# A Hyena and SwiGLU encoder layer: reordering the joint between the output projection and the first SwiGLU pair

## The chip, the core and the metric

The kernel runs on one core of one Trainium2 chip. The metric is the device time of one execution in microseconds; a kernel's time is the median of several runs. TensorE does matmuls and transposes, VectorE elementwise work on two operands, ScalarE activations and copies, GpSimd (POOL in the profile) elementwise work on SBUF and the issue of software DMAs, SyncE (SP) the issue of the other DMAs.

## The reference, cut to what matters

One layer (DEPTH is 1) over 1024 tokens of width 1024, in float32:

```
h = rmsnorm(x, norm_mix)
z = short_conv(h @ w_in + b_in, conv_w, conv_b);  x0, x1, v = split(z, 3)
s = v * x1
y = fft_convolution(s, implicit_filter) + s * skip
x = x + (y * x0) @ w_out + b_out
x = x + (silu(n @ w_gate) * (n @ w_up)) @ w_down      # n = rmsnorm(x, norm_ffn)
out = rmsnorm(x, norm_final)
```

The hidden width of the SwiGLU part is 2816.

## The kernel before, in words

**Numbers.** Every large matmul is done in three products of rounded parts. An operand is split into a high part (a cast to fp32r) and a low part (the value less the high part), and the terms (high, high), (high, low), (low, high) are summed in PSUM (`TERMS`). A low part is made in one of three ways: a subtraction on VectorE; a subtraction on GpSimd; or `low_dma` (L148 to L150): ScalarE writes minus the high part to the low tile, then POOL's queue issues a DMA that adds the source onto it. `split_dma` (L152) is the cast and then `low_dma`; `early_op` (L1302) calls it for a weight.

**Output projection.** `wos[h][k // 2]` are the split weights of column half h, `u2[part][th]` the split input, one K tile k of 128 rows each. `out_part(m, ks, terms)` (L925) adds the K tiles ks to the first column half of row tiles m and m + 4. K tiles 0 to 5 are done in an earlier stretch; K tile 6 (the seventh) is done at L1008 to L1012 with `inverse_mm` of the last Hyena block between its pieces; tile 7 closes. Within the seventh K tile each row tile's three terms follow one another, and the second term reads the low part of weights `wos[0][3]`, a `low_dma`.

**The loop of the joint (L1310).** It goes over the second column half in the order of rows `seq = (0, 4, 1, 5, 2, 3, 6, 7)`. Step n: TensorE computes the half for row tile j = seq[n] (24 matmuls), then transposes row tile seq[n-1] (`turn`, L1292; the result, `tp`, lies in one of two PSUM tiles). VectorE and ScalarE do, in this order: `x1_half(j)` (L1035: add to x1, square with sum on ScalarE, store to `xd` on SP's queue); `post_late()`, what the step before left over; `normed(j)` (L1078: `norm_begin` L1063 and `norm_end` L1068, which scales both halves of x1 in place; the second half must wait until the store of L1045 has read it); `post(seq[n-1])`, the split of the transposed tile.

**The split of a transposed tile.** Rows 0 to 3 are left tiles (`top_left`, L1091): ScalarE casts the high part from PSUM to u2, copies the tile to x1, and for tiles 0 to 2 `low_dma` makes the low part; for tile 3 VectorE subtracts it, in `post_late`. Rows 4 to 7 are right tiles (class `Right`, L1103): besides their own parts T4 and B22 they give the sums T1, T2, T3 of a Strassen scheme, each split (`high`, `low`). For rows 4 and 5 `top_sums` (L1166) does all of it in the loop; for rows 6 and 7 (`r6`, `r7`) the steps are written out after the loop.

**The SwiGLU units.** A `Unit` (L1197) is one block of 256 columns of the gate (`ug`) or up weights (`uu_`): four raw quarters a11, a12, a21, a22, loaded on SP into slots that x1 tiles 0, 1, 4 and 5 held, sums s0 to s3 of them, and seven products of 12 matmuls: a (p1) and b (p2) into pa, f into pb, g into pc, e into pd, then d on top of pc and c on top of pd. pc and pd are the halves of one PSUM tile, `dc`. `p1_out` (L1249) copies pa to SBUF on ScalarE before p2 adds to it. `w_op` (L1191) splits a weight operand with ScalarE and VectorE. `end_products` (L1274) first adds pd to a running sum (L1275) and then calls for d and c; `end_sums` reads all of dc.

**The joint after the loop (L1347 to L1408)** is a hand-written order of r6, r7, both first units and `normed(7)`. The early weight parts are `pre` (a11 of both units) and `pq` (a12 of both).

**What sets the order.** In the joint the order of TensorE, VectorE and ScalarE is the program's own (`manual_schedule`, L1306). SP and POOL are ordered there by the framework's planner; up to L1051 they are by hand too. Every queue works in order.

Of the kernel before, what the change touches and what calls it, by code (L numbers as in the profile page):

```python
# [13 lines left out]
ALU = mybir.AluOpType  # L14
# [88 lines left out]
def hyena_ffn_kernel(ctx: ExitStack, tc: tile.TileContext, a: dict, out: bass.AP):  # L103
# [15 lines left out]
    def slot(tag, name, shape=(1024,), dt=F32):  # L119
        return sb.tile([P, *shape], dt, tag=tag, name=name)  # L120
# [27 lines left out]
    def low_dma(hi, lo, src):  # L148
        S.activation(lo, hi.bitcast(F32), AF.Copy, scale=-1.0)  # L149
        G.dma_start(lo.bitcast(F32), src, accum_op=ALU.add)  # L150
# [774 lines left out]
    def out_part(m, ks, terms=range(len(TERMS))):  # L925
        for k in ks:
            for q, j in enumerate(PAIRS[m]):
                out_mm(po[m][:, q * 512 : (q + 1) * 512], 0, j, k, terms)
# [76 lines left out]
    wo_load(1, 3, "hs")  # L1005
    wo_split(1, 1)
    x1_load(5)
    out_part(0, (6,))  # L1008
    out_part(1, (6,), (0, 1))
    inverse_mm(b)  # L1010
    out_part(1, (6,), (2,))
    out_part(2, (6,))  # L1012
    finish(b)
    gate(b)
# [63 lines left out]
    def normed(j):  # L1078
        norm_begin(j)
        norm_end(j)  # L1080
# [10 lines left out]
    def top_left(m, pt):  # L1091
        ms = cols_of(m)
        S.copy(u2[0][0][:, :, ms], pt)
        xt = x1[m].rearrange("p (k m) -> p k m", k=NB)
        S.copy(xt, pt)
        if m < 3:
            low_dma(u2[0][0][:, :, ms], u2[1][0][:, :, ms], xt)
            return lambda: None
        return lambda: V.tensor_tensor(
            u2[1][0][:, :, ms], pt, u2[0][0][:, :, ms].bitcast(F32), ALU.subtract  # L1100
        )
# [95 lines left out]
    class Unit:  # L1197
# [54 lines left out]
        def p2(u, t=None, ks=range(4)):  # L1252
            u.product(u.pa, "b", u.a12, "B21", False, t, ks)

        def sums(u, eng):
            eng.tensor_tensor(u.s[0], u.a21, u.a22, ALU.add)
            eng.tensor_tensor(u.s[1], u.s[0], u.a11, ALU.subtract)

        def sum3(u):
            V.tensor_tensor(u.s[2], u.a11, u.a21, ALU.subtract)  # L1260
# [31 lines left out]
    def turn(j):  # L1292
        turns[j] = turned(j)
# [4 lines left out]
    def post_late():  # L1298
        while late:
            late.pop(0)()  # L1300

    def early_op(t, src):  # L1302
        split_dma(t[:, 0], t[:, 1], src)
        return t

    with tc.manual_schedule(  # L1306
        engines={mybir.EngineType.PE, mybir.EngineType.DVE, mybir.EngineType.Activation}
    ):
        pts = {}
        for n, j in enumerate(seq):  # L1310
            if n % 4 < 2:
                pts[n % 2] = mm_psum(f"po1{n}")
            hf = n // 2 % 2
            o = pts[n % 2][:, hf * 512 : (hf + 1) * 512]
            for k in range(NB):
                out_mm(o, 1, j, k)
            if n == 1:
                t_op("T1", "ab_g", ("gg0",))
                t_op("T2", "cr", ("fwd01",))
                t_op("T3", "whl1", ("hs", "wt"))  # L1320
            if 1 <= n <= 6:
                turn(seq[n - 1])
            if n == 7:
                turn(6)
                pq = slot("ss", "pq", (2, 2, 4, P), F32R)
                early_op(pq[:, 0], ug.a12)
            x1_half(j, 1, o)
            if n == 6:
                early_op(pre[:, 1], uu_.a11)
            if n < 7:  # L1330
                post_late()
                normed(j)
            if 1 <= n <= 6:
                post(seq[n - 1])
            if n == 3:
                ug = Unit(0, wg, "wg")
            if n == 4:
                uu_ = Unit(0, wu, "wu")
                pre = slot("whl0", "pre", (2, 2, 4, P), F32R)
            if n == 5:  # L1340
                early_op(pre[:, 0], ug.a11)
            if n == 6:
                post_late()
                ug.s_tag = "ab_d"
                ug.split_sum_tiles()
                ug.sums(V)
        ug.begin(True)  # L1347
        uu_.begin(True)
        r6 = Right(2, turns[6])
        r6.sums12()  # L1350
        norm_begin(7)
        r6.sum3()
        r6.high("T2")
        r6.b22_high()
        norm_end(7)
        ug.p1(pre[:, 0])
        r6.high("T3")
        r6.low("T3", None)
        early_op(pq[:, 1], uu_.a12)
        r6.low("T2", V)  # L1360
        r6.b22_low()
        ug.p1_out()
        ug.early = {"f": w_op("wg0f", ug.s[1])}
        uu_.p1(pre[:, 1])
        turn(7)
        r6.sum4()
        r6.high("T1")
        r6.low("T1", None)
        uu_.p1_out()
        r7 = Right(3, turns[7])  # L1370
        r7.sums12()
        r7.sum3()
        ug.p2(pq[:, 0])
        uu_.p2(pq[:, 1], (0, 1))
        r6.t4_high()
        r6.t4_low(None)
        r7.part("T2", V)
        r7.part("T3", V)
        ug.sum3()
        ug.early["g"] = w_op("wg0g", ug.s[2])  # L1380
        r7.part("T1", V)
        r7.sum4()
        ug.early["e"] = w_op("wg0e", ug.s[0])
        ug.product(ug.pb, "f", None, "T2", True, ug.early["f"])
        V.tensor_tensor(ug.uu[:, 1], ug.uu[:, 0], ug.pb, ALU.add)
        r7.t4_high()
        r7.t4_low(None)
        r7.b22_high()
        r7.b22_low()
        ug.product(ug.pc, "g", None, "T3", True, ug.early["g"])  # L1390
        uu_.p2(pq[:, 1], (2, 3))
        V.tensor_tensor(ug.uu[:, 2], ug.uu[:, 1], ug.pc, ALU.add)
        ug.product(ug.pd, "e", None, "T1", True, ug.early["e"])
        ug.sum4()
        g0 = slot("inv", "g0", (4, 512))
        ug.early["d"] = w_op("wg0d", ug.a22)
        uu_.sum_tiles()
        uu_.sums(V)
        uu_.early["f"] = w_op("wu0f", uu_.s[1])
        ug.end_products(g0[:, 1:4])  # L1400
        uu_.sum3()
        uu_.early["g"] = w_op("wu0g", uu_.s[2])
        S.activation(g0[:, 0], ug.pa, AF.Silu)
        ug.end_sums(g0[:, 1:4])
        uu_.sum4()
        uu_.product(uu_.pb, "f", None, "T2", True, uu_.early["f"])
        V.tensor_tensor(uu_.uu[:, 1], uu_.uu[:, 0], uu_.pb, ALU.add)
        uu_.product(uu_.pc, "g", None, "T3", True, uu_.early["g"])  # L1408

    held = []  # L1410
# [1 line left out]
    def pair(i, ug=None, uu_=None):  # L1412
        early = ug is not None
        g = g0 if early else slot("inv", f"g{i}", (4, 512))
        if not early:
            ug = Unit(i, wg, "wg")
            ug.begin()
            ug.p1()
            ug.p1_out()
            ug.sums(V)  # L1420
            ug.middle()
            ug.p2()
            S.activation(g[:, 0], ug.pa, AF.Silu)
            ug.end(g[:, 1:4])
        S.activation(g[:, 1:4], g[:, 1:4], AF.Silu)
        if not early:
            uu_ = Unit(i, wu, "wu")
            uu_.begin()
            uu_.p1()
            uu_.p1_out()  # L1430
            uu_.sums(V)
            uu_.middle()
            uu_.p2()
        else:
            uu_.middle(True)
        uc = slot("whl0", f"uc{i}", (3, 512))
        V.tensor_tensor(g[:, 0], g[:, 0], uu_.pa, ALU.mult)  # L1437
        uu_.end(uc, early)
        V.tensor_tensor(g[:, 1:4], g[:, 1:4], uc, ALU.mult)
        inner(i, g, store)  # L1440
# [16 lines left out]
    def last_pair(i):  # L1457
        g = slot("inv", f"g{i}", (4, 512))
        ug, uu = Unit(i, wg, "wg"), Unit(i, wu, "wu")
        ug.begin()  # L1460
        uu.begin()
        ug.p1()
        ug.p1_out()
        ug.sums(V)
        uu.p1()
        uu.p1_out()
        ug.product(ug.pb, "f", ug.s[1], "T2", True)
        V.tensor_tensor(ug.uu[:, 1], ug.uu[:, 0], ug.pb, ALU.add)
        ug.sum3()
        ug.product(ug.pc, "g", ug.s[2], "T3", True)  # L1470
        V.tensor_tensor(ug.uu[:, 2], ug.uu[:, 1], ug.pc, ALU.add)
        ug.p2()
        S.activation(g[:, 0], ug.pa, AF.Silu)
        ug.product(ug.pd, "e", ug.s[0], "T1", True)
        uu.sums(V)
        uu.product(uu.pb, "f", uu.s[1], "T2", True)
        V.tensor_tensor(uu.uu[:, 1], uu.uu[:, 0], uu.pb, ALU.add)
        ug.end(g[:, 1:4])
        S.activation(g[:, 1:4], g[:, 1:4], AF.Silu)
        uu.sum3()  # L1480
        uu.product(uu.pc, "g", uu.s[2], "T3", True)
        V.tensor_tensor(uu.uu[:, 2], uu.uu[:, 1], uu.pc, ALU.add)
        uu.p2()
        V.tensor_tensor(g[:, 0], g[:, 0], uu.pa, ALU.mult)
        uu.product(uu.pd, "e", uu.s[0], "T1", True)
        uc = slot("whl0", f"uc{i}", (3, 512))
        uu.end(uc)
        V.tensor_tensor(g[:, 1:4], g[:, 1:4], uc, ALU.mult)
        inner(i, g, lambda *x: held.append(x))
# [211 lines left out]
```

## Time and profile before

| what | value |
|---|---|
| median of 3 runs (lowest to highest) | 1176.32 us (1175.88 to 1178.87) |
| time of the profiled execution | 1177.2 us |
| its span, first to last instruction | 1175.4 us |
| mean granted TensorE clock | 0.996 |
| ScalarE busy, share of the span | 44% |
| DMA moved | 172.95 MB, mean 147 GB/s |

The profile is one execution. A row of the timeline gives start, duration, engine, line, operation, output and inputs, shape and count; in brackets stands how long the engine had been idle before it and what released it. A row of the waits gives an engine and its instruction, what it waited for, the total, how often, and the longest. The row of a window gives, after its ends and its length, for each engine the busy time and the number of instructions, then the granted clock, the share of the DMA engines and GB/s. A row of DMA issues gives the queue, the count, the size and the median time to landing. "PEld" is TensorE's weight load, "SPq" and "POOLq" the issuing queues.

### The profile page before, as it was taken

Reading aid. Unit: us, or ns where it says so; the run is one execution under the profiler, and the core shown is the slowest. Engines: PE = TensorE matmul, PEld = TensorE weight load, DVE = VectorE, ACT = ScalarE, POOL = GpSimd, SP = SyncE. Lnnn points to the kernel's source line nnn. Section 1 sums busy time; section 2 is a strip of 40 time slices with the busy share of each in tenths; the row PEclk is TensorE's granted clock in tenths of the full one; section 3 lists DMA queues with packets and bytes.
Section 4 is the critical chain, followed back from the end, with each engine's and each line's share of the span. In section 5 each row is a group of like instructions: output and inputs, shape, how many; then the busy total and the mean of one; then the engine's idle time right before and its main releaser. Section 6 shows DMA issues by size and latency. Waiting matters only on the chain.

```text
span 1175.4 us, 15154 instructions
## 1 busy us (share of the span) xinstructions
PE 1151.6 (98%) x5714; PEld 970.0 (83%) x5714; DVE 870.8 (74%) x1389; ACT 522.3 (44%) x829; POOL 155.1 (13%) x218
## 2 busy tenths in 40 slices
PE   8999999999999999988999999999999999999997
PEld 6889898898988888876888888888888788788886
DVE  7688989889898895477756676666566567955675
ACT  8563553545446474365333233323333243334445
POOL 0010211112011141052001110111011110110100
PEclk9999999999999999999999999999999999999999
DMA  7456778776674799576223332324133269833323
GB/s 240 145 120 144 141 163 170 159 166 155 129 161 100 195 245 298 148 138 105 96 101 120 105 115 69 130 90 135 56 124 108 75 231 374 297 117 96 99 81 144
DMA packets 105818, 172.95 MB, mean 147 GB/s; under 512 B 7181, under 2 KB 65933, under 8 KB 105616
## 3 DMA queue, kind: packets, MB, share of 16 engines
q0 software_dynamic: 30080, 81.02, 30.5%
q1 hardware_dynamic: 75517, 90.70, 23.3%
q8 instruction: 45, 0.74, 0.2%
q10 hardware_dynamic: 146, 0.27, 0.1%
q14 instruction: 30, 0.24, 0.1%
HBM read 101.96 MB, written 40.11 MB: 121 GB/s over the span
## 4 chain that ended last, share of the span: by engine, by line
PE 85%; DVE 7%; DMA 6%; ACT 1%; issue 1%; POOL 0%; DVEq 0%; POOLq 0%; ACTq 0%; SPq 0%
PE z L140 20%; PE bx L1560 8%; PE po L914 3%; PE bz L1560 3%; PE by L1560 3%; PE pg L541 2%; PE pp L614 2%; PE pg L540 2%; DMA wd<-in_ffn_w_down_dram 2%; DMA xd<-x 1%; DMA wohl<-wo 1%; PE py L653 1%; PE py L654 1%; PE z L366 1%; PE z L693 1%; PE wu9dc L1237 1%
## 5 line engine op out<-in xcount | busy, mean ns | idle before, releaser
L140 PE MATMUL z<-uh,whl 128*128 128x512 f32 x704 | 195.4, 392 | 0.0
L140 PEld LDWEIGHTS z<-uh,whl 128*128 128x128 f32 x704 | 130.1, 188 | 25.6
L1560 PE MATMUL bx<-wop,hop 128*128 128x512 f32 x480 | 110.1, 389 | 0.8 <-DVE hop L130 0.8
L140 PE MATMUL z<-ul,whl 128*128 128x512 f32 x352 | 108.8, 390 | 0.0
L1560 PEld LDWEIGHTS bx<-wop,hop 128*128 128x128 f32 x480 | 90.0, 188 | 19.9 <-DVE hop L130 1.2
L130 DVE TENSOR_TENSOR hop<-hrp,hop 128x1024 fp32r<-128x1024 f32 (+1 forms) x40 | 45.0, 1130 | 52.3 <-ACT hop L129 52.3
L129 ACT CAST hop<-hrp 128x1024 fp32r<-128x1024 f32 (+1 forms) x40 | 38.9, 977 | 96.9 <-PE bx L1560 32.5
L140 PEld LDWEIGHTS z<-ul,whl 128*128 128x128 f32 x352 | 66.1, 188 | 14.1
L914 PE MATMUL po<-wohl,uh 128*128 128x512 f32 x256 | 75.1, 397 | 0.8 <-DMA wohl<-wo 0.7
L1030 POOL DMA_DIRECT2D hd<-g x40 | 21.6, 543 | 320.2 <-DVE g L1437 188.3
L1560 PE MATMUL by<-wop,hop 128*128 128x512 f32 x264 | 60.2, 389 | 0.0
L1560 PEld LDWEIGHTS by<-wop,hop 128*128 128x128 f32 x264 | 49.6, 188 | 10.3
L914 PEld LDWEIGHTS po<-wohl,uh 128*128 128x128 f32 x256 | 48.0, 190 | 11.3 <-DMA wohl<-wo 1.2
L194 ACT CAST whl<-wt 128x1024 fp32r<-128x1024 f32 x24 | 25.2, 1050 | 68.2 <-PE z L140 64.7
L130 DVE TENSOR_TENSOR wop<-wd,wop 128x512 fp32r<-128x512 f32 x73 | 47.7, 687 | 3.5 <-ACT wop L129 3.5
L150 POOL DMA_DIRECT2D whl<-wt x24 | 20.8, 866 | 218.9 <-ACT whl L149 131.0
L541 PE MATMUL pg<-hw,fwd 128*128 128x128 f32 x256 | 49.5, 275 | 0.0
L540 PE MATMUL pg<-hw,fwd 128*128 128x128 f32 x256 | 49.5, 275 | 0.0
L129 ACT CAST wop<-wd 128x512 fp32r<-128x512 f32 x73 | 42.2, 617 | 14.1 <-PE by L1560 4.9
L1030 POOL DMA_DIRECT2D hrp<-hd x42 | 22.3, 532 | 184.7 <-DVE hop L130 160.4
L914 PE MATMUL po<-wohl,ul 128*128 128x512 f32 x128 | 44.4, 393 | 0.0
L540 PEld LDWEIGHTS pg<-hw,fwd 128*128 128x128 f32 x256 | 39.4, 192 | 0.6
(1593 smaller groups left out, 2836.0 us busy)
## 6 DMA issues: line engine op xcount, KB each, us to landing
hrp<-hd POOLq DMA_DIRECT2D x35, 512.0 KB, 4.0
wt<-in_hy_w_in_dram SPq DMA_DIRECT2D x24, 512.0 KB, 5.0
whl<-wt POOLq DMA_DIRECT2D x24, 512.0 KB, 4.6
wgr<-in_ffn_w_gate_dram SPq DMA_DIRECT2D x22, 512.0 KB, 4.3
wur<-in_ffn_w_up_dram SPq DMA_DIRECT2D x22, 512.0 KB, 3.7
wd<-in_ffn_w_down_dram SPq DMA_DIRECT2D x44, 256.0 KB, 6.6
hd<-g POOLq DMA_DIRECT2D x40, 256.0 KB, 2.4
hd<-sx POOLq DMA_DIRECT2D x30, 256.0 KB, 2.8
```

The source lines that it names most:

```text
L129: S.copy(hi, src)
L130: (eng or V).tensor_tensor(lo, src, hi.bitcast(F32), ALU.subtract)
L140: T.matmul(pt[:, h * 512 : (h + 1) * 512], w[wi], u2[ui][h][:, k, :], start=first and ti == 0, stop=last and ti == len(TERMS) - 1,)
L150: G.dma_start(lo.bitcast(F32), src, accum_op=ALU.add)
L194: S.copy(whl[:, 0], w_raw[n])
L366: T.matmul(z_psum[n][:, lo:hi], w_hl[n][wi][:, k, :], u2[ui][lo // 512][:, k, lo % 512 : (hi - 1) % 512 + 1], start=k == 0 and ti == 0 and ...
L540: T.matmul(o, fwd[r][:, j, :], f.hw[:, j, 0, :], start=True, stop=False)
L541: T.matmul(o, fwd[2 * r][:, jj, :], f.hw[:, jj, 1, :], start=False, stop=True)
L614: T.matmul(pt[:, j * P : (j + 1) * P], fwd[r][:, j, :], z.sT[:, j, :], start=True, stop=True)
L914: T.matmul(o, u2[yi][th][:, k, m * P : (m + 1) * P], wos[h][k // 2][wi][:, k % 2, :], start=(k == 0 and ti == 0), stop=(k == NB - 1 and ti ...
L1030: G.dma_start(dst, src)
L1560: T.matmul(pt, ho[hi_][:, x, q * P : (q + 1) * P], wo_[wi][:, x, :], start=fresh and first and x == 0 and ti == 0, stop=last and x == n - ...
```

## The change

- Seventh K tile: terms 0 and 2 (high weights) of row pairs 0 and 1 come first, then term 1 (low weights) of pair 0, then `inverse_mm`, then term 1 of pair 1.
- `top_left`: the low parts of tiles 0 to 2 are made like that of tile 3, by VectorE from PSUM in the next step's `post_late`. The copy to x1 stays.
- `pre` of the gate is split at n = 4 (was 5), `pre` of the up unit at n = 5 (was 6, ahead of the normed step). The cast of uu's a12 is at n = 7, its low part right after `norm_begin(7)`.
- `sums` is cut into `sum1` and `sum2`, both on VectorE. Those of ug are at n = 5 and at n = 6 (they were at the end of n = 6); `sum3` of ug is the first after the loop.
- After the loop: r6's T1 comes ahead of its T3, r6's T4 and r7's first sums ahead of the up unit's `p1_out`; r7's T4 low part is VectorE's instead of a DMA's, and r7's B22 follows.
- The closing order is e, d, f of uu, c, g of uu (it was e, d, c, f, g), and the sum of pd stands behind d's emission, not ahead of it. The operand of c is split early.

The diff, without the renamed calls of the later units (`ug.sums(V)` becomes `ug.sums()`):

```
-    out_part(0, (6,))
-    out_part(1, (6,), (0, 1))
+    out_part(0, (6,), (0, 2))
+    out_part(1, (6,), (0, 2))
+    out_part(0, (6,), (1,))
     inverse_mm(b)
-    out_part(1, (6,), (2,))
+    out_part(1, (6,), (1,))
     out_part(2, (6,))
...
         S.copy(u2[0][0][:, :, ms], pt)
-        xt = x1[m].rearrange("p (k m) -> p k m", k=NB)
-        S.copy(xt, pt)
-        if m < 3:
-            low_dma(u2[0][0][:, :, ms], u2[1][0][:, :, ms], xt)
-            return lambda: None
+        S.copy(x1[m].rearrange("p (k m) -> p k m", k=NB), pt)
         return lambda: V.tensor_tensor(
             u2[1][0][:, :, ms], pt, u2[0][0][:, :, ms].bitcast(F32), ALU.subtract
         )
...
-        def sums(u, eng):
-            eng.tensor_tensor(u.s[0], u.a21, u.a22, ALU.add)
-            eng.tensor_tensor(u.s[1], u.s[0], u.a11, ALU.subtract)
+        def sum1(u):
+            V.tensor_tensor(u.s[0], u.a21, u.a22, ALU.add)
+
+        def sum2(u):
+            V.tensor_tensor(u.s[1], u.s[0], u.a11, ALU.subtract)
+
+        def sums(u):
+            u.sum1()
+            u.sum2()
...
                 early_op(pq[:, 0], ug.a12)
+                S.copy(pq[:, 1, 0], uu_.a12)
             x1_half(j, 1, o)
-            if n == 6:
-                early_op(pre[:, 1], uu_.a11)
             if n < 7:
                 post_late()
+                if n == 6:
+                    ug.sum2()
                 normed(j)
...
                 pre = slot("whl0", "pre", (2, 2, 4, P), F32R)
+                early_op(pre[:, 0], ug.a11)
             if n == 5:
-                early_op(pre[:, 0], ug.a11)
+                early_op(pre[:, 1], uu_.a11)
+                ug.s_tag = "ab_d"
+                ug.split_sum_tiles()
+                ug.sum1()
             if n == 6:
                 post_late()
-                ug.s_tag = "ab_d"
-                ug.split_sum_tiles()
-                ug.sums(V)
         ug.begin(True)
         uu_.begin(True)
+        ug.sum3()
+        norm_begin(7)
+        low_dma(pq[:, 1, 0], pq[:, 1, 1], uu_.a12)
         r6 = Right(2, turns[6])
         r6.sums12()
-        norm_begin(7)
-        r6.sum3()
+        norm_end(7)
         r6.high("T2")
         r6.b22_high()
-        norm_end(7)
+        r6.high("T1")
+        r6.low("T1", None)
         ug.p1(pre[:, 0])
+        uu_.p1(pre[:, 1])
+        r6.sum3()
+        r6.low("T2", V)
+        ug.p1_out()
+        ug.early = {"f": w_op("wg0f", ug.s[1])}
+        turn(7)
+        r6.sum4()
         r6.high("T3")
         r6.low("T3", None)
-        early_op(pq[:, 1], uu_.a12)
-        r6.low("T2", V)
         r6.b22_low()
-        ug.p1_out()
-        ug.early = {"f": w_op("wg0f", ug.s[1])}
-        uu_.p1(pre[:, 1])
-        turn(7)
-        r6.sum4()
-        r6.high("T1")
-        r6.low("T1", None)
-        uu_.p1_out()
         r7 = Right(3, turns[7])
         r7.sums12()
+        r6.t4_high()
+        r6.t4_low(None)
+        uu_.p1_out()
         r7.sum3()
         ug.p2(pq[:, 0])
         uu_.p2(pq[:, 1], (0, 1))
-        r6.t4_high()
-        r6.t4_low(None)
         r7.part("T2", V)
+        ug.early["g"] = w_op("wg0g", ug.s[2])
         r7.part("T3", V)
-        ug.sum3()
-        ug.early["g"] = w_op("wg0g", ug.s[2])
         r7.part("T1", V)
         r7.sum4()
         ug.early["e"] = w_op("wg0e", ug.s[0])
         ug.product(ug.pb, "f", None, "T2", True, ug.early["f"])
+        r7.t4_high()
+        r7.b22_high()
+        r7.t4_low(V)
         V.tensor_tensor(ug.uu[:, 1], ug.uu[:, 0], ug.pb, ALU.add)
-        r7.t4_high()
-        r7.t4_low(None)
-        r7.b22_high()
         r7.b22_low()
         ug.product(ug.pc, "g", None, "T3", True, ug.early["g"])
         uu_.p2(pq[:, 1], (2, 3))
         V.tensor_tensor(ug.uu[:, 2], ug.uu[:, 1], ug.pc, ALU.add)
         ug.product(ug.pd, "e", None, "T1", True, ug.early["e"])
+        ug.early["d"] = w_op("wg0d", ug.a22)
         ug.sum4()
-        g0 = slot("inv", "g0", (4, 512))
-        ug.early["d"] = w_op("wg0d", ug.a22)
         uu_.sum_tiles()
-        uu_.sums(V)
+        uu_.sums()
         uu_.early["f"] = w_op("wu0f", uu_.s[1])
-        ug.end_products(g0[:, 1:4])
+        ug.early["c"] = w_op("wg0c", ug.s[3])
         uu_.sum3()
         uu_.early["g"] = w_op("wu0g", uu_.s[2])
+        g0 = slot("inv", "g0", (4, 512))
+        ug.product(ug.pc, "d", None, "T4", False, ug.early["d"])
+        V.tensor_tensor(g0[:, 3], ug.uu[:, 2], ug.pd, ALU.add)
+        uu_.product(uu_.pb, "f", None, "T2", True, uu_.early["f"])
         S.activation(g0[:, 0], ug.pa, AF.Silu)
+        uu_.sum4()
+        V.tensor_tensor(uu_.uu[:, 1], uu_.uu[:, 0], uu_.pb, ALU.add)
+        ug.product(ug.pd, "c", None, "B22", False, ug.early["c"])
         ug.end_sums(g0[:, 1:4])
-        uu_.sum4()
-        uu_.product(uu_.pb, "f", None, "T2", True, uu_.early["f"])
-        V.tensor_tensor(uu_.uu[:, 1], uu_.uu[:, 0], uu_.pb, ALU.add)
         uu_.product(uu_.pc, "g", None, "T3", True, uu_.early["g"])
```

More of the change, by code (lines that the diff above doesn't have):

```diff
@@ L1419, in pair @@
             ug.p1_out()
-            ug.sums(V)
+            ug.sums()
             ug.middle()
@@ L1430, in pair @@
             uu_.p1_out()
-            uu_.sums(V)
+            uu_.sums()
             uu_.middle()
@@ L1463, in last_pair @@
         ug.p1_out()
-        ug.sums(V)
+        ug.sums()
         uu.p1()
@@ L1474, in last_pair @@
         ug.product(ug.pd, "e", ug.s[0], "T1", True)
-        uu.sums(V)
+        uu.sums()
         uu.product(uu.pb, "f", uu.s[1], "T2", True)
```

## The prediction

> **What bounds the kernel now.** I read the page's first part, then TensorE's waits, then the timeline of the joint (the end of the output projection and the first SwiGLU pair), then who sets each wait.
>
> ```profile
> span 1175.4 us, 15154 instructions
> PE 1151.6 (98%) x5714; PEld 970.0 (83%) x5714; DVE 870.8 (74%) x1389; ACT 522.3 (44%) x829; POOL 155.1 (13%) x218
> ```
>
> TensorE sets the time. A change that leaves its products alone can win only its waits. Those in the joint, from the list of TensorE's waits:
>
> ```profile
> PE wu0ab L1237 <- DMA pq<-wur: 2.6, 1, 2.6
> PE tp L1085 <- issue: 2.2, 1, 2.2
> ...
> PE wg0dc L1237 <- DVE g L1275: 1.3, 1, 1.3
> PE wg0ab L1237 <- DMA pre<-wgr: 1.2, 1, 1.2
> ...
> PE tp L1085 <- DVE x L1076: 0.9, 1, 0.9
> ...
> PE wg0ab L1237 <- ACT wg0u L1250: 0.8, 1, 0.8
> PE po L914 <- DMA wohl<-wo: 0.7, 1, 0.7
> ```
>
> The chain and TensorE's timeline give what they cost together:
>
> ```profile
> 496.07 0.60 PE L1085 MATMUL tp<-ident,x 128*128 128x128 f32 x4
> ...
> 505.87 1.74 PE L1085 MATMUL tp<-ident,x 128*128 128x128 f32 x8 [2.18 <-issue]
> ...
> 513.87 1.04 PE L1085 MATMUL tp<-ident,x 128*128 128x128 f32 x8
> ...
> 520.22 1.03 PE L1085 MATMUL tp<-ident,x 128*128 128x128 f32 x8
> ```
>
> ```profile
> 564.56 2.72 PE wu0dc L1237 x12
> ```
>
> A loop step (eight K tiles and a turn) takes 520.22 - 513.87 = 6.35, a product of 12 matmuls 2.72, one matmul 0.227, so a turn some 0.8. From 496.07, where turn(1) is due, to the end of the up unit's g at 567.28 there are four steps, two turns and eleven products: 25.4 + 1.6 + 29.9 = 56.9. It took 71.2, so 14.3 are lost. The six waits listed for that stretch make 9.0. Two slow spells follow the two longest:
>
> ```profile
> 505.80:509.60 3.80, 3.73 (x14) 3.16 (x15) 2.60 (x8) 1.97 (x5) 1.56 (x1) 0.55 0.39 94
> 542.40:547.70 5.30, 5.22 (x16) 4.13 (x17) 3.35 (x6) 2.97 (x6) 0.00 (x0) 0.68 1.18 183
> ...
> 529.30:532.00 2.70, 2.67 (x12) 2.20 (x13) 1.40 (x3) 1.20 (x3) 0.00 (x0) 1.00 1.20 177
> ```
>
> The column ahead of the last two is the granted clock. After the waits of 2.2 and 2.6 it falls to 0.55 and 0.68; after the 1.2 it stays at 1.00. The step from 505.87 takes 8.00 (to 513.87), 1.65 too long, and the f product 543.52 to 547.85 (rows below), 1.61 too long. That leaves 2.0 over six waits: draining and refilling, 0.35 each. [...]
>
> Most of the first two waits is a store. Vector must not overwrite the second half of x1 before its store has read it:
>
> ```profile
> 490.65 6.06 DMA xd<-x
> ...
> 515.52 4.18 DMA xd<-x
> ...
> 521.13 4.54 DMA xd<-x
> ```
>
> ```profile
> q0 software_dynamic: 562, 0.29, 131.8%
> ```
>
> The last row is the window from 492 to 494: only the software queue, that is the left tile's low part (512 KB, added by DMA), moves, at full share. The store, issued at 490.65, waits behind it. The shortest landing of these stores is 2.0:
>
> ```profile
> DMA to landing us min/median/max: 2.0/5.1/5.3
> ```
>
> **The change part by part.**
>
> Seventh K tile. The second matmul waits for the weights' low half.
>
> ```profile
> 448.16 0.39 PE L914 MATMUL po<-wohl,uh 128*128 128x512 f32 x1
> 449.27 0.50 PE L914 MATMUL po<-wohl,uh 128*128 128x512 f32 x1 [0.72 <-DMA wohl<-wo]
> ```
>
> Now eight matmuls that read high weights come first: 8 x 0.227 = 1.8, over the 1.1 to the landing. Gain 0.7; the inverse products behind it start earlier by as much, as VectorE has only to answer with rn. Were the cover gone, 0.7 would stay.
>
> Low parts of left tiles 0 to 2. Removed: three ScalarE passes and three 512 KB DMAs on POOL's queue; added, three VectorE subtractions.
>
> ```profile
> 489.94 0.69 DVE L1037 TENSOR_TENSOR x<-x,po 128x512 f32<-128x512 f32 x1 [2.20 <-PE po L914]
> 491.41 0.16 DVE L1065 SCALAR_TENSOR_TENSOR rq<-sq 128x1 f32<-128x1 f32 x1 [0.79 <-ACT jq L1038]
> ...
> 496.74 0.75 DVE L1076 SCALAR_TENSOR_TENSOR x<-x,rq,gffn 128x512 f32<-128x512 f32 x1 [3.37 <-DMA xd<-x]
> ...
> 505.01 1.42 DVE L1076 SCALAR_TENSOR_TENSOR x<-x,rq,gffn 128x512 f32<-128x512 f32 x2
> ...
> 526.36 1.22 DVE L1099 TENSOR_TENSOR ul<-tp,uh 128x1024 fp32r<-128x1024 f32 x1
> ```
>
> One costs 1.22 (the fourth tile's). It stands between L1037 and L1065, where 0.79 is idle: 0.43 later. Tile 1's normed second half then starts near 493.7, not 496.74, if its store lands in under 3; all that VectorE does up to the normed tile 5 follows 3.05 earlier. Turn(1) is due at 496.07: its 0.9 goes. Turn(5) is due at 496.07 + 6.35 = 502.4; the first half it needs is done at 505.72 - 3.05 = 502.7, the second 0.7 later. Some 0.7 of wait is left, and I count the 1.65 of slow clock as gone, as 1.2 left the clock whole.
>
> Next is tile 3, where VectorE, not the DMA, is late. The early split of the gate's a11 now stands on ScalarE ahead of tile 3's square:
>
> ```profile
> 519.22 0.62 ACT L153 CAST pre<-wgr 128x512 fp32r<-128x512 f32 x1
> 519.87 0.63 ACT L149 ACTIVATE pre<-pre 128x512 fp32r<-128x512 f32 x1
> ```
>
> That is 1.25 before a square for which VectorE waits. Queued behind on VectorE is all of normed(3); TensorE waits for it in turn(3). Carrying the rows on from tile 5 (low part + 0.43, no store wait), b22_low ends near 512.9, the square's sum comes at 514.2, the normed halves at 516.75 and 517.4. TensorE is at turn(3) by 515.7: a new wait of some 1.4, between 0 (ScalarE ahead of what I carry on) and 2.6 (the two added passes, 1.25, slip once more). At turn(6) (TensorE 523.5) the normed tile is there at 523.0, after low(2), sum1 and sum2 (0.7 each by L1037's row, of the same width); p1's low part of tile 3 by 524.2. So p1 starts near 524.3, where it started at 527.34.
>
> Holding a turned tile's PSUM until VectorE has subtracted costs nothing as long as VectorE is at it within a step: the bank is wanted two turns, 12.7 us, later. SP's loads into the slots of x1 tiles 0 and 1 lose one wait, that for the left tile's DMA, and can go sooner; the stores keep their places on SP, tile 3's behind such a load, which is why I give its store the 4.2 of before rather than 2.
>
> Weight parts sooner. p1 waited 1.2 for its low part, uu's p2 2.6 and a slow spell:
>
> ```profile
> pre<-wgr POOLq DMA_DIRECT2D x1, 256.0 KB, 8.5
> ...
> pq<-wur POOLq DMA_DIRECT2D x1, 256.0 KB, 5.3
> ```
>
> Pre's two DMAs now leave POOL near 514 and 518.4, with no left tile ahead; even at 8.5 they land by 526.9, and the second is wanted at 527.4. The pq of uu leaves at 527, before T1's and T3's DMAs instead of between them, and lands by 533, wanted at 535. Both waits and the 1.61 go. Its cast now stands ahead of tile 7's square: 0.6 on ScalarE while VectorE is still busy with tile 3's low part, so nothing; were it not, 0.6 more at turn(7). On POOL's queue r6's T1 now goes ahead of its T3: T3's pieces leave near 533.5 and 534.5, and g wants them at 540. R7's T4 low becomes a pass of VectorE (0.7) while f runs, and one DMA of POOL less; d wants it at 546.
>
> The tail's ScalarE order. New here is who lets p2 start:
>
> ```profile
> 535.83 0.57 ACT L1250 COPY wg0u<-wg0ab 128x512 f32<-128x512 f32 x1
> ...
> 538.01 0.57 ACT L1250 COPY wu0u<-wu0ab 128x512 f32<-128x512 f32 x1
> ```
>
> Tile 7's half ends on VectorE at 524.85; sum3 follows, the square's sum, r6's copy on ScalarE, then L1117 and L1118 (0.7 each) by 528.6. Ug's p1_out now stands behind four passes of 0.6 that begin there (T2, B22, T1, T1's low): it ends near 531.4. Norm_end(7) ends at 530.7, so turn(7), due at 529.7, loses 0.65; p2 waits 0.3 more. Uu's p1_out moves behind six passes after that (f, T3, T3's low, r7's copy, r6's T4 pair; 3.6): it ends at 535.5, while TensorE is done with p2 at 534.25. A wait of 1.35 takes the place of the 2.6 one (0 to 2.5 by the same 1.25 either way). R7's T2 low, wanted by f at 537.0, ends at 536.75.
>
> D ahead of the closing sum, f between. D waited for L1275:
>
> ```profile
> 543.52 0.51 PE L1237 MATMUL wg0ab<-T2h,wg0f 128*128 128x512 f32 x1
> ...
> 547.85 0.40 PE L1237 MATMUL wg0dc<-T3h,wg0g 128*128 128x512 f32 x1
> ...
> 556.13 0.47 PE L1237 MATMUL wg0dc<-uh,wg0d 128*128 128x512 f32 x1 [1.30 <-DVE g L1275]
> ```
>
> Now d follows e at once, 1.3 gained. C must still wait for that sum, but two products, 5.4, cover it; the operands' lows are done by 548.2, wanted at 552. If the sum were late, its 0.7 would come back.
>
> Sum: of 14.3 lost, new waits 0.7 + 1.4 + 0.65 + 0.3 + 1.35 = 4.4 and four times 0.35 stay, 5.8. Gain 14.3 - 5.8 + 0.7 = 9.2. The profiled execution took 1177.2 (1.8 around its span), so 1168.0; it stood 0.9 above the median of the three runs: 1167.1. After the joint TensorE waits in the list only 0.8 and 0.7, so the lead is kept.
>
> **The rivals.** All waits go: my carried times on ScalarE are too late and nothing replaces them. 14.3 + 0.7 from 1176.3 is 1161.3; with one small wait kept, 1162. For it: the 0.3 to 1.4 are small differences; against: VectorE's busy time in the loop,
>
> ```profile
> 496.07:527.34 31.27, 28.22 (x137) 23.24 (x136) 23.26 (x46) 20.53 (x37) 14.61 (x13) 0.95 0.67 137
> ```
>
> 23.3 (third pair) and two lows more, 25.7, would have to fit into 524.3 - 496.07 = 28.2 with its waits for ScalarE.
>
> Two new waits pass 2 us: turn(3) and uu's p2 each grow by 0.7 and bring a slow spell of 1.65: 1167.1 + 4.7 = 1171.8. For it: the 0.55 row, and 1.4 is not far from 2.2.
>
> The stores don't come sooner: the gate's and up's loads, right behind or ahead on SP, hold them instead. Then the loop wins nothing, pays part of its lows, and only tail and K tile win: about 1175, no change. The row at full share of the software queue alone speaks against.
>
> Slower: VectorE's queue becomes the end. With the stores' waits unchanged, three lows and the split ahead of the square make 3.66 + 1.25 = 4.9 on the way from L1037 to r7's T2 low, which f needs:
>
> ```profile
> 541.20 0.69 DVE L1140 TENSOR_TENSOR T2l<-tta,T2h 128x512 fp32r<-128x512 f32 x1
> ```
>
> 541.89 + 4.9 = 546.8, where f began at 543.52: 3.3 late; a further slow spell 1.65, less 1.4 at d: 1176.3 + 3.5 = 1179.8. It decides once VectorE's queue grows by over 1.6.
>
> **How the numbers follow.** Forecast 0.64 (1164.5 to 1170 by its bounds), all waits gone 0.12, two long waits 0.14, stores unchanged 0.06, VectorE the end 0.04. The range from 1161 to 1172 takes in the first three and leaves out the last two, and what of the third lies beyond its sum. Over 0.3% (3.5 us, about what can be told from no change) faster: 0.64 + 0.12 + 0.14 = 0.90; within 0.06; slower 0.04.
>
> **What would show it.** Right: no software DMA between 490 and 496; the stores land in 2 to 4.5; no wait on pq, pre, or L1275; granted clock 1.00 across the joint; small waits at turn(5), turn(3), turn(7) and uu's p2, the last on wu0u's copy. Wrong: a clock of 0.5 to 0.7 in the joint, a wait on x L1076 over 2 us, or TensorE stopping behind the joint.

## The result and the profile after

The changed kernel takes 1165.54 us (median of 4 runs, 1165.29 to 1166.17) against 1176.57 (4 runs, 1175.88 to 1178.87) of the kernel before: a ratio of 0.9906, 95% interval 0.9893 to 0.9918, 11.0 us. The forecast was 1167.1, 9.2 faster. The profiled execution took 1165.29 us.

The page's first part, after:

```profile
span 1163.4 us, 15135 instructions
PE 1148.5 (99%) x5714; PEld 968.0 (83%) x5714; DVE 873.1 (75%) x1393; ACT 519.4 (45%) x825; POOL 149.3 (13%) x214
```

TensorE's instructions are as many as before. What remains of its waits in the joint:

```profile
PE wu0ab L1234 <- ACT wu0u L1247: 0.9, 1, 0.9
PE tp L1086 <- PE po L914: 0.8, 1, 0.8
...
PE py L653 <- DVE rn L663: 0.3, 1, 0.3
PE tp L1086 <- DVE x L1077: 0.2, 1, 0.2
```

The six waits of before between turn(1) and the up unit's g, and that for the low weights, are gone. Three new ones make 1.9: 0.9 at the up unit's second product (p2), 0.8 at turn(3), 0.2 at turn(5). The list puts the one at turn(3) down to TensorE's own `po`, which had long been done; what came last there is the normed tile 3 on VectorE (below). Where the time went shows best in three stretches: turn(1) to turn(2), turn(2) to turn(6), turn(6) to the first product of the second gate unit, which follows the up unit's g. Columns: ends, length, busy time (and instructions) of TensorE, its weight loads, VectorE, ScalarE and GpSimd, then granted clock, DMA share, GB/s. Before:

```profile
496.07:513.87 17.80, 14.75 (x66) 11.79 (x65) 14.57 (x28) 9.68 (x19) 6.74 (x6) 0.90 0.61 142
513.87:526.55 12.68, 12.68 (x65) 10.66 (x64) 7.90 (x18) 10.73 (x19) 7.84 (x7) 1.00 0.70 130
526.55:567.10 40.55, 34.68 (x149) 27.47 (x148) 31.54 (x53) 21.67 (x39) 9.52 (x8) 0.96 0.67 114
```

After:

```profile
494.95:508.39 13.44, 13.13 (x66) 10.57 (x65) 11.80 (x24) 6.89 (x15) 4.46 (x4) 1.00 0.41 117
508.39:522.25 13.86, 13.07 (x65) 10.57 (x64) 11.26 (x24) 11.05 (x21) 6.97 (x6) 1.00 0.59 115
522.25:555.76 33.51, 32.56 (x149) 26.34 (x148) 29.92 (x53) 19.95 (x38) 8.16 (x7) 1.00 0.61 118
```

The first stretch gains 4.4, the second loses 1.2, the third gains 7.0: 10.2 together. The clock is 1.00 throughout, where it had been 0.90 and 0.96. Turn(1) itself starts 1.1 earlier (494.95 for 496.07), nearly all of it from the seventh K tile. The first inverse product behind that tile, before and after:

```profile
451.98 0.49 PE L653 MATMUL py<-inv,vv 128*128 128x128 f32 x2 [0.26 <-DVE rn L663]
```

```profile
450.87 0.49 PE L653 MATMUL py<-inv,vv 128*128 128x128 f32 x2 [0.26 <-DVE rn L663]
```

Together, 10.2 and 1.1 are 11.3 of the 12.0 by which the span fell; the rest lies outside the joint.

The chain in the loop after:

```profile
489.53 2.24 DMA xd<-x
491.77 1.40 DVE x L1077 x2
...
497.11 4.47 DMA xd<-x
```

Tile 1's store lands after 2.24, where it took 6.06, and the normed tile follows at once. Tile 5's still takes 4.47: SP has issued 512 KB of the gate's load just ahead of it (at 496.54), and from 497 to 501.6 only SP's queue moves, 0.79 MB, the load and the store together.

### The profile page after: what moved, and what is told of

It reads as the page before. It is cut to its first block, busy times and chain, and to the rows that moved or that the text cites. A ratio compares the mean times of both kernels' runs of the same rounds, so it can differ in the third digit from the quotient of the medians.

```text
span 1163.4 us, 15135 instructions
## 1 busy us (share of the span) xinstructions
PE 1148.5 (99%) x5714; PEld 968.0 (83%) x5714; DVE 873.1 (75%) x1393; ACT 519.4 (45%) x825; POOL 149.3 (13%) x214
## 4 chain that ended last, share of the span: by engine, by line
PE 84%; DVE 9%; DMA 3%; ACT 1%; issue 1%; SPq 0%; POOL 0%; DVEq 0%; POOLq 0%; ACTq 0%
PE z L140 20%; PE bx L1568 7%; PE po L914 3%; PE bz L1568 3%; PE by L1568 3%; PE pp L614 2%; PE pg L541 2%; PE pg L540 2%; DVE wd L1622 1%; PE py L653 1%; DMA wd<-in_ffn_w_down_dram 1%; PE py L654 1%; PE z L366 1%; PE z L693 1%; PE wu9dc L1234 1%
## 5 line engine op out<-in xcount | busy, mean ns | idle before, releaser
L140 PEld LDWEIGHTS z<-ul,whl 128*128 128x128 f32 x352 | 66.1, 188 | 14.1
L1568 PE MATMUL by<-wop,hop 128*128 128x512 f32 x264 | 60.2, 389 | 0.0
```

The lines of the kernel that those rows point to most:

```text
L140: T.matmul(pt[:, h * 512 : (h + 1) * 512], w[wi], u2[ui][h][:, k, :], start=first and ti == 0, stop=last and ti == len(TERMS) - 1,)
L1568: T.matmul(pt, ho[hi_][:, x, q * P : (q + 1) * P], wo_[wi][:, x, :], start=fresh and first and x == 0 and ti == 0, stop=last and x == n - ...
```

## The experiments

The first two columns are the timed median and its ratio to the kernel before, with the interval; the last is the length from turn(1) to the second gate unit's first product in the profiled execution (71.0 before, 60.8 after; 56.9 without any wait). The runs were timed in four sessions, in which the kernel before took 1176.57, 1176.84, 1177.52 and 1177.62, so rows far apart compare better by ratio than by time.

| kernel | us | ratio | stretch, us |
|---|---|---|---|
| changed | 1165.54 | 0.9906 [0.9893, 0.9918] | 60.8 |
| low parts by DMA again | 1168.83 | 0.9931 [0.9917, 0.9946] | 65.7 |
| low parts on VectorE alone | 1169.95 | 0.9940 [0.9926, 0.9955] | 64.4 |
| three plain copies by software DMA added | 1165.45 | 0.9902 [0.9888, 0.9917] | 60.7 |
| three adding software DMAs added | 1168.82 | 0.9936 [0.9913, 0.9960] | 64.3 |
| low parts on GpSimd | 1169.30 | 0.9937 [0.9921, 0.9954] | 64.1 |
| old K tile order | 1166.83 | 0.9904 [0.9891, 0.9918] | 60.5 |
| old closing order | 1172.88 | 0.9959 [0.9946, 0.9972] | 67.6 |
| old weight parts and tail | 1167.15 | 0.9911 [0.9897, 0.9925] | 63.0 |
| gate's a11 split in a gap | 1164.23 | 0.9882 [0.9867, 0.9897] | 60.2 |
| same, tail reordered | 1165.54 | 0.9899 [0.9882, 0.9916] | 60.2 |
| VectorE 1.4 longer ahead of turn(5) | 1166.36 | 0.9902 [0.9879, 0.9924] | 61.2 |
| VectorE 2.8 longer ahead of turn(5) | 1166.69 | 0.9905 [0.9883, 0.9927] | 62.2 |

The theory was that the left tile's software DMA held the store that the normed tile waits for. The rivals were that the loads on SP held it, and that what the change freed was ScalarE's time or the planner's order.

**The low parts by DMA again.** In the changed kernel:

```
-        S.copy(x1[m].rearrange("p (k m) -> p k m", k=NB), pt)
+        xt = x1[m].rearrange("p (k m) -> p k m", k=NB)
+        S.copy(xt, pt)
+        if m < 3:
+            low_dma(u2[0][0][:, :, ms], u2[1][0][:, :, ms], xt)
+            return lambda: None
```

> The changed kernel, but the low parts of left tiles 0 to 2 are again made by ScalarE and a software DMA. Theory (the software DMA holds the store that the normed tile waits for): the store of tile 1 lands after 5 to 6 us, the waits at turn(1) and turn(5) return with the slow spell behind the second, and the time is 4.5 to 6 over the changed kernel's 1165.5, so 1170 to 1171.5. Rival (the loads on SP hold the stores): the stores land in 2 to 4.5 as after, and the time is within 1.5 of 1165.5.

The chain and TensorE's turns:

```profile
489.68 6.05 DMA xd<-x
```

```profile
496.57 0.66 PE L1086 MATMUL tp<-ident,x 128*128 128x128 f32 x4 [0.87 <-DVE x L1077]
504.89 1.88 PE L1086 MATMUL tp<-ident,x 128*128 128x128 f32 x8 [2.19 <-issue]
```

Store and both waits are back as in the kernel before, nearly to the hundredth. The time rose by 3.3, less than the 4.5 to 6 expected: with TensorE later, the changed kernel's own wait at turn(3) is not there. SP issues its stores and loads in the same order in this kernel, in the changed one and in the one before, so the loads are not what holds the store.

**The low parts alone.** The same edit the other way round, in the kernel before.

> The kernel before with one part of the change alone: the low parts of left tiles 0 to 2 on VectorE. Theory: the stores land in 2 to 3, the waits at turn(1) and turn(5) fall to under 1 and the slow spell there goes, while the waits of the tail (weight parts, d) stay or grow; 4 to 6 faster than before, so 1170.5 to 1172.5. Rival (VectorE's three subtractions cost what the stores give): 1175 to 1177.

The gain of 6.9 (from 1176.84, the kernel before in the same session) is a little over the upper end, and tile 1's store lands early here too:

```profile
490.46 2.24 DMA xd<-x
```

This part alone gives more than half of the whole, and with all the others present it still gives 3.3: the parts overlap. What it leaves in the tail, from TensorE's timeline:

```profile
536.37 0.73 PE L1233 MATMUL wu0ab<-uh,pq 128*128 128x512 f32 x2 [1.54 <-DMA pq<-wur]
...
549.31 0.47 PE L1233 MATMUL wg0dc<-uh,wg0d 128*128 128x512 f32 x1 [1.75 <-DVE g L1271]
```

The wait for pq has shrunk from 2.6 without its order being touched, and the slow spell behind it is gone (f takes 2.72, 537.40 to 540.12, where it took 4.33); the wait of d has grown.

**A transfer without its passes.** To the changed kernel, three plain copies:

```
+    SCR = [yd.tile([P, NB, P], F32, tag=f"scr{m}", name=f"scr{m}") for m in range(3)]
...
-        S.copy(x1[m].rearrange("p (k m) -> p k m", k=NB), pt)
+        xt = x1[m].rearrange("p (k m) -> p k m", k=NB)
+        S.copy(xt, pt)
+        if m < 3:
+            G.dma_start(SCR[m], xt)
```

> The changed kernel plus three software DMAs of 512 KB that copy the turned left tiles 0 to 2 from SBUF to scratch in HBM; nothing waits for them but the slot they read, and ScalarE has no pass more. Theory: the transfer alone is enough, the store of tile 1 lands after 4 or more and the waits at turn(1) and turn(5) return in part, 1 to 5 over the changed kernel, so 1166.5 to 1170.5. Rival (what the change freed is ScalarE's time, or the planner's order): stores land in 2 to 3 and the time is within 0.5 of 1165.5.

No time was lost. The first copy left POOL at 486.69 and was over before tile 1's store went out (2.23 to landing). The second left at 501.58, landed after 3.0 and ran beside tile 2's store, and there both queues moved. Packets, megabytes and share from 503 to 504.5:

```profile
q0 software_dynamic: 116, 0.41, 68.3%
q1 hardware_dynamic: 70, 0.14, 31.0%
```

The normed tile behind that store took 1.52, where it took 1.41. So a plain copy of 512 KB, in 4 KB pieces (0.41 MB in 116 packets), did not hold the store, and the theory, which took any transfer to be enough, is wrong there. The DMA that the change removed adds, in 512-byte pieces (0.29 MB in 562 packets from 492 to 494). The second try does both (the scratch holds no value that is read later):

```
+        if m < 3:
+            G.dma_start(
+                xb[:, m].rearrange("p (k m) -> p k m", k=NB),
+                u2[0][0][:, :, ms].bitcast(F32),
+                accum_op=ALU.add,
+            )
```

> The changed kernel plus three adding software DMAs in 512-byte pieces, like the ones it did away with: the high part of left tiles 0 to 2 is added onto a scratch in HBM that is no longer read. No pass of ScalarE comes with it and nothing waits for it. Theory (the adding transfer alone holds the store): it runs some 4 us from about 489, the store of tile 1 lands after 4.5 to 6 instead of 2.2, waits at turn(1) and turn(5) come back, 2 to 4 over the changed kernel, 1167.5 to 1169.5. Rival (the ScalarE passes or the planner's order freed the loop): the store lands in 2 to 3, within 0.5 of 1165.5.

The time is as expected, at other places. The first transfer leaves POOL at 485.62, 2.0 sooner than with the low parts by DMA again (487.61), as it needs only the cast; so it holds tile 1's store by less (3.08 in place of 2.24). The second meets tile 2's. The queues' packets, megabytes and share from 503 to 506, the chain, and VectorE behind it:

```profile
q0 software_dynamic: 922, 0.47, 136.1%
q1 hardware_dynamic: 2, 0.00, 0.4%
```

```profile
503.12 4.64 DMA xd<-x
```

```profile
507.79 0.75 DVE L1077 SCALAR_TENSOR_TENSOR x<-x,rq,gffn 128x512 f32<-128x512 f32 x1 [1.69 <-DMA xd<-x]
```

The store issued at 503.12 gets next to nothing of the engines in those 3 us, and VectorE stands for 1.69. TensorE's wait comes at turn(3), with the clock at 0.62 behind it:

```profile
517.56 1.94 PE L1086 MATMUL tp<-ident,x 128*128 128x128 f32 x8 [2.53 <-issue]
```

No pass of ScalarE was added, and SP's order is that of the changed kernel, so the adding transfer alone is enough. Whether it is the adding or the small pieces that matters, no run tells.

**The low parts on GpSimd.**

```
-        S.copy(x1[m].rearrange("p (k m) -> p k m", k=NB), pt)
+        xt = x1[m].rearrange("p (k m) -> p k m", k=NB)
+        S.copy(xt, pt)
+        if m < 3:
+            G.tensor_tensor(
+                u2[1][0][:, :, ms], xt, u2[0][0][:, :, ms].bitcast(F32), ALU.subtract
+            )
+            return lambda: None
```

> The changed kernel, with the low parts of left tiles 0 to 2 made by GpSimd from the copy in SBUF. Theory: only the DMA had to go, so any engine does; VectorE is three passes of 1.22 shorter and the waits at turn(5) and turn(3) fall by 0.4 or more: 1164 to 1165.5. Rival (GpSimd's passes of some 2.5 hold VectorE's small norm passes, which took 0.78 instead of 0.16 beside it): waits at turn(5) and turn(3) grow, 1166 to 1169.

The rival holds at turn(5), where the wait grows; at turn(3) it does not, and the time is 0.3 over the rival's range. GpSimd's pass of tile 1's low part, then VectorE and TensorE in that time:

```profile
501.13 2.50 POOL L1098 TENSOR_TENSOR ul<-x,uh 128x1024 fp32r<-128x1024 f32 x1 [0.90 <-ACT x L1096]
```

```profile
500.68 3.51 DVE L1077 SCALAR_TENSOR_TENSOR x<-x,rq,gffn 128x512 f32<-128x512 f32 x2
```

```profile
504.25 0.79 PE L1086 MATMUL tp<-ident,x 128*128 128x128 f32 x4 [2.08 <-DVE x L1077]
```

The two halves of the normed tile take 3.51, where the same pair takes 1.63 in the changed kernel and tile 1's 1.41, and end 0.56 after GpSimd's pass. So it is the wide pass that is held, more than the small ones that the rival names. Turn(5) waits 2.08 for it and the clock falls to 0.56. What of the two passes makes the one hold the other, no run shows. The change's subtractions are VectorE's own and take 1.22 each, with no elementwise pass of GpSimd beside them.

**The other parts, each undone.** The K tile:

```
-    out_part(0, (6,), (0, 2))
-    out_part(1, (6,), (0, 2))
-    out_part(0, (6,), (1,))
+    out_part(0, (6,))
+    out_part(1, (6,), (0, 1))
     inverse_mm(b)
-    out_part(1, (6,), (1,))
+    out_part(1, (6,), (2,))
```

> The changed kernel with the seventh K tile's terms in the old order. Theory: the 0.7 wait for the low weights with its drain is back and nothing later takes it up: 0.7 to 1.1 over the changed kernel, 1166.2 to 1166.7. Rival (VectorE in the loop is the end there and takes up what is lost ahead of it): within 0.3 of 1165.5.

The median is 0.1 over the theory's upper end, while the ratio can't tell it from the changed kernel. In the profiled executions turn(1) comes 0.87 later (495.82) and the second gate unit 0.6 later, a little having been taken up in between: near the theory's lower end.

The closing order:

```
-            u.product(u.pd, "c", u.s[3], "B22", False)
+            u.product(u.pd, "c", u.s[3], "B22", False, u.early.get("c"))
...
-        ug.product(ug.pc, "d", None, "T4", False, ug.early["d"])
-        V.tensor_tensor(g0[:, 3], ug.uu[:, 2], ug.pd, ALU.add)
-        uu_.product(uu_.pb, "f", None, "T2", True, uu_.early["f"])
+        ug.end_products(g0[:, 1:4])
         S.activation(g0[:, 0], ug.pa, AF.Silu)
-        uu_.sum4()
-        V.tensor_tensor(uu_.uu[:, 1], uu_.uu[:, 0], uu_.pb, ALU.add)
-        ug.product(ug.pd, "c", None, "B22", False, ug.early["c"])
         ug.end_sums(g0[:, 1:4])
+        uu_.sum4()
+        uu_.product(uu_.pb, "f", None, "T2", True, uu_.early["f"])
+        V.tensor_tensor(uu_.uu[:, 1], uu_.uu[:, 0], uu_.pb, ALU.add)
```

> The changed kernel with the old closing order: sum of pd ahead of d, then d, c, f of uu. Theory: d waits again for that sum, 1.3 to 1.7 longer: 1166.8 to 1167.3. Rival (the operands' lows, not the sum, come last, and d would wait without it): c or f of uu waits instead and the time is within 0.5 of 1165.5 or over 1168.

The time is 7.3 over (6.2 by the ratio). That is the rival's range, but not its reason, as neither c nor f of uu waits. TensorE's timeline, then VectorE's:

```profile
549.87 0.76 PE L1234 MATMUL wg0dc<-uh,wg0d 128*128 128x512 f32 x1 [4.97 <-DVE g L1278]
```

```profile
544.82 0.69 DVE L130 TENSOR_TENSOR wu0f<-wu0s,wu0f 128x512 fp32r<-128x512 f32 x1 [0.74 <-ACT wu0f L129]
...
549.04 0.68 DVE L1278 TENSOR_TENSOR g<-wg0u,wg0dc 128x512 f32<-128x512 f32 x1
```

D waits for the sum, as the theory has it, but the sum stands behind weight operands on VectorE: e ended near 544.9, and the sum began at 549.04. Between the split of f and that sum VectorE makes three splits and three sums (545.43 to 549.04), all of which stand behind the sum in the kernel before (555.90 to 559.60). So this run prices d behind a queue that is longer than it was, not the old place; and the wait of 4.97 brought a slow spell (0.50 in the 3.8 behind it). The old place is priced by the next pair.

The weight parts and the tail as before, with the other three parts:

> The kernel before with the K tile order, the low parts on VectorE and the closing order: the weight parts, the sums and the order of r6 and r7 stay as before. Theory: VectorE's low parts alone gained 6.9, the two others add 1.0 and 1.7 to 2.0: 1166.8 to 1167.4, with the wait for pq of uu (1.5 with low parts alone) kept. Rival (the earlier weight parts carry the gain of the tail): 1168.5 or more.

Its edit is the K tile, `top_left` and closing order of the diff, in the kernel before. 1167.15 is in the range, and the wait for pq is 1.53. The stretch is 63.0 where low parts alone have 64.4: the closing order is worth 1.4. Against the changed kernel it is 2.2 longer, though its turn(3) comes without the new wait. So the weight parts and the tail are worth some 2 in the profiles, net of what they cost at turn(3); the ratios' intervals overlap, so the times do not show it. (This profiled execution, 1169.12, is the slowest of its four, with a wait of 1.55 near its end, outside the stretch.)

**Where the changed kernel still waits.** At turn(3) VectorE idled for ScalarE:

```profile
512.91 0.85 DVE L1066 SCALAR_TENSOR_TENSOR rq<-sq 128x1 f32<-128x1 f32 x1 [1.11 <-ACT jq L1039]
```

The edit puts the split where ScalarE idles:

```
+            if n == 4:
+                pre = slot("whl0", "pre", (2, 2, 4, P), F32R)
+                early_op(pre[:, 0], ug.a11)
             if 1 <= n <= 6:
                 post(seq[n - 1])
...
                 uu_ = Unit(0, wu, "wu")
-                pre = slot("whl0", "pre", (2, 2, 4, P), F32R)
-                early_op(pre[:, 0], ug.a11)
```

> The changed kernel with the gate's a11 split ahead of tile 5's sums on ScalarE, where it sits idle for some 3 us, instead of behind them and ahead of tile 3's square. Theory (that split on ScalarE delays the square and so turn(3)): VectorE's idle 1.1 before tile 3's norm goes, the wait at turn(3) of 0.8 goes, 0.7 to 1.2 faster than the changed kernel: 1164.3 to 1164.9. Rival (VectorE's own queue makes turn(3) late): within 0.3 of 1165.5.

The idle time before that row is gone, and so is the listed wait at turn(3). But a later small pass of the norm now falls beside a pass of GpSimd and takes 0.78, where it took 0.16:

```profile
512.73 1.28 POOL L1153 TENSOR_TENSOR ul<-tt,uh 128x512 fp32r<-128x512 f32 x1
```

```profile
513.25 0.78 DVE L1072 SCALAR_TENSOR_TENSOR rq<-rq 128x1 f32<-128x1 f32 x1
```

So of VectorE's 1.1 only 0.5 reaches TensorE: turn(2) to turn(6) takes 13.36, for 13.86, and 12.7 without any wait. The stretch is 0.7 shorter. 1164.23 is the lowest median of the study, but the ratio's interval overlaps that of the changed kernel.

Then the tail, on top of that:

```
-        r6.high("T3")
-        r6.low("T3", None)
-        r6.b22_low()
         r7 = Right(3, turns[7])
         r7.sums12()
-        r6.t4_high()
-        r6.t4_low(None)
         uu_.p1_out()
+        r6.high("T3")
+        r6.low("T3", None)
         r7.sum3()
+        r6.b22_low()
...
         r7.part("T2", V)
+        r6.t4_high()
+        r6.t4_low(None)
```

> As the run before, and in the tail r7's first sums and the up unit's copy of pa stand ahead of r6's T3 and T4 on ScalarE, with r6's T4 and B22 low behind r7's T2. Theory (six ScalarE passes ahead of that copy make the wait of 0.9 at p2 of the up unit): the wait goes, f is then held by r7's T2 low at some 0.5; 0.6 to 1.0 faster than the run before: 1163.5 to 1164.2. Rival (T3's or T4's low part by DMA now lands too late and g or d waits): within 0.3 of the run before, or slower.

The wait for wu0u goes, and f waits 0.55 for T2's low and e 0.22 for a sum in its place: a stretch of 60.2 against 60.2. No gain can be shown.

**How long a wait cools the clock.** At n == 3, ahead of `post_late()`: `for _ in range(2): late[0]()`, then `range(4)`.

> The changed kernel with VectorE's B22 low part of tile 4 done three times instead of once (same values), 1.2 to 1.4 longer ahead of turn(5). Theory (a wait of 2.2 or more cools TensorE's clock, one of 1.3 does not): the wait at turn(5) is 1.4 to 1.8, the clock stays at 1.00, 1.0 to 1.4 over the changed kernel. Rival (the fall depends on how waits add up over a stretch, not on one): the clock falls after this wait or at turn(3), 2.5 or more over.

> As the run before, but five times instead of once, 2.4 to 2.8 longer ahead of turn(5). Theory: the wait at turn(5) is 2.6 to 3.1, the granted clock falls to 0.5 to 0.6 for some 3.5 us behind it and the step takes about 1.6 longer; as turn(3)'s wait is then taken up, 2.5 to 3.5 over the changed kernel. [...]

Both waits came out shorter than expected, at 0.74 and 1.73 on TensorE; the second one's row:

```profile
503.19 1.27 PE L1086 MATMUL tp<-ident,x 128*128 128x128 f32 x8 [1.73 <-issue]
```

The clock stayed at 1.00 after either, and the second's step took 6.60. So neither reached what it was to test. Of 2.8 us of added work only 1.4 (60.8 to 62.2) showed: while the repeats ran, the store landed and GpSimd finished, so that waits of the changed kernel fell into the same time (behind the four repeats two small passes of the norm take 0.15 and 0.16, where they took 0.78 each, and the two halves 1.41, where they took 1.63).

## Why the prediction was right, step by step

- **The store behind the software DMA**: right, and shown. Taking the transfer away brings the landing from 6.06 to 2.24 in two kernels; an adding one to another place, which nothing waits for, brings a held store and a wait back. A plain copy does not.
- **Turn(1) and turn(5)**: 0.9 gone, and some 0.7 of turn(5) left. By the first stretch two steps took 13.44 for 12.7, so 0.7. The slow spell is gone.
- **Turn(3)**: 1.4 and a drain forecast, 1.2 lost by the second stretch (13.86 for 12.7). The reason given, the split ahead of the square, is shown for 0.5 of it. The other 0.7 stays with the split in a gap, where VectorE is done with tile 3 at 516.02 and turn(3), due at 515.03, wants the second half 0.4 later; 0.6 is lost with the old weight parts too (13.29). So VectorE is late there without the split as well, which the forecast did not tell apart.
- **Tail**: waits for pre, pq and L1275 gone; the wait on wu0u's copy in their place, 0.9 listed and 1.2 lost, for 1.35 (535.5 less 534.25 is 1.25). Turn(7) lost 0.5 for 0.65, and p2 did not wait for ug's copy (0.3 forecast). Turn(7), p2 of the gate and p2 of the up unit:

```profile
528.61 1.27 PE L1086 MATMUL tp<-ident,x 128*128 128x128 f32 x8
529.92 0.50 PE L1234 MATMUL wg0ab<-uh,pq 128*128 128x512 f32 x1
...
533.85 0.50 PE L1234 MATMUL wu0ab<-uh,pq 128*128 128x512 f32 x1 [0.91 <-ACT wu0u L1247]
```

- **The closing order**: 1.4 by the pair of runs, for 1.3 to 1.4.
- **The K tile**: 0.7 forecast, 1.0 measured (py 1.1 earlier, of which 0.1 came from earlier on): the drain of a removed wait comes with it.

The term that was mis-sized is the last of the sum, "four times 0.35 stay". The new waits had been reckoned from when TensorE was due to when it could go on, and that holds most of the drain already: at turn(3) the list has 0.79, from due (514.72) to start is 0.95, and all that was lost is 1.16. The four places lost 0.7 + 1.2 + 0.5 + 1.2 = 3.6, drain included, and the stretch after holds 3.9 over 56.9, not 5.8. Of these 1.9, 1.4 are that term; the rest is p2's 0.3 and waits that came out shorter. Against that the loss before was 14.1 and not 14.3: g begins at 564.40 on TensorE's timeline, and 567.28 was taken from the chain's 564.56. With the K tile's 0.3 the sum would have been 9.2 + 1.9 + 0.3 - 0.2 = 11.2, for the 11.3 of the trace.

The rival of two long waits did not come: no wait left in the joint passes 0.91. Four of the runs pass 2 us there and pay with a slow spell (clock 0.50 to 0.62, last section). That a wait of over 2 us brings one was read in the joint alone, though: the same profile of the kernel before has a wait of 2.14 at 16.09 with the clock at 1.00 behind it (last section). The rival that VectorE becomes the end needs stores that land no sooner; they landed sooner, and with low parts alone, three passes more on VectorE, the waits at turn(1) and turn(5) fell to 0.2 and less.

## What to carry to other kernels

A store that a later in-place pass must wait for can be on the path, also where what holds it is another queue's: here it landed after 6.06 beside an adding DMA in 512-byte pieces and after 2.24 without. Look which transfers share the DMA engines at that moment. When a wait goes, walk on in each engine's order to the next instruction that is late, and count a wait from due time to start once, drain included. What is moved forward in a queue costs at the first instruction behind it that somebody waits for: ahead of the square the split cost VectorE 1.1 and TensorE 0.5, in ScalarE's gap nothing.

## What the runs showed of the hardware

- An adding software DMA of 512 KB in 512-byte pieces kept a store on the other queue out: 0.4% of the engines beside 136.1%, over 3 us (922 packets, 0.47 MB). A plain copy of 512 KB in 4 KB pieces did not: 31.0% beside 68.3%, over 1.5 us (116 packets, 0.41 MB). How the engines divide their time between the two queues, no run shows.
- Behind waits in the joint of 2.08, 2.19, 2.53 and 4.97 the clock is 0.56, 0.55, 0.62 and 0.50 over 3.8 us; behind that of 1.73 it is 1.00, and behind that of 1.75 (low parts on VectorE alone) four products take 11.0, for four times 2.72. But the length alone does not decide: at the start of the program, ahead of the transposes of the input, TensorE waits 2.14 in the kernel before and 2.21 in the kernel with the split in a gap, and the clock stays at 1.00. What else decides is open. Three windows, with the columns of the three stretches above: VectorE 2.8 longer (1.73), low parts on GpSimd (2.08), and the split in a gap, with its wait:

```profile
503.10:506.90 3.80, 3.71 (x20) 3.04 (x21) 3.39 (x9) 1.65 (x5) 0.00 (x0) 1.00 0.37 110
```

```profile
504.20:508.00 3.80, 3.75 (x12) 3.09 (x13) 2.54 (x8) 1.40 (x4) 0.00 (x0) 0.56 0.58 165
```

```profile
16.52:20.32 3.80, 3.65 (x29) 3.36 (x30) 3.54 (x7) 2.98 (x4) 0.00 (x0) 1.00 0.94 216
```

```profile
16.52 1.97 PE L300 MATMUL tp<-ident,xn 128*128 128x128 f32 x16 [2.21 <-DVE ul L310]
```

In the first two TensorE is as busy, with 20 products in the one and 12 in the other. In the kernel before the spell costs 1.65 behind the wait of 2.2 and 1.61 behind that of 2.6.
